# Router logits from the raw sums, gathers by four experts and three one-shot load places in a two-layer MoE block

## The chip, the cores and the metric

The kernel runs on one core of a Trainium2 chip. The metric is the device time of one execution in microseconds; 2232.28 us is the median of three runs of the kernel before (2230.65 to 2234.52).

## The reference, cut to what matters

256 tokens of 1024 channels go through a first block (half feed-forwards, neighbourhood attention with an mLSTM, spatial gating) and then through two layers of the block that the change touches. Each layer mixes the tokens, adds and normalises, sends every token to 2 of 16 experts, adds and normalises again:

```python
x = layer_norm_2(ALPHA * x + mix, ln_g[l, 0], ln_b[l, 0])
ffn = routed_moe(x, router_w, router_b, moe_w_gate[l], moe_w_up[l], moe_w_down[l])
x = layer_norm_2(ALPHA * x + ffn, ln_g[l, 1], ln_b[l, 1])

def routed_moe(x, ...):
    aff = sigmoid(xt @ router_w)                 # 256 x 16
    sel = aff + router_b                         # best of 4 groups of 4 experts, in it the top 2
    ...
    y = y + gates[:, e:e+1] * ((silu(xt @ w_gate[e]) * (xt @ w_up[e])) @ w_down[e])
```

`layer_norm_2` takes the mean and the variance over the 1024 channels, then gain and shift. Everything is f32.

## The kernel before

The tokens lie in two tiles t of 128, the channels in 8 blocks k of 128. A layer of the second block runs so.

**w_o projection** (`N.down`, `rows_out`, L184 to L187). The mixer's output times w_o, in split single-pass products, accumulates in four banks `yacc` (two halves n of 512 channels for each t). Tile 0's last matmuls come before tile 1's, 24 for each. For each finished tile `norm2` (L766) is called: DVE adds `x = ALPHA x + yacc` by halves (L772), gathers statistics (L773, L761), takes 1/sqrt by three steps of Newton (`rsq`, L216 to L225) and writes `xn` (L776).

**Router** (`moe`, L1081). PE transposes `xn` (L255). ACT (L1219, the first four k) and DVE (L1222, the last four) copy it out of PSUM as `xT` with gain and shift. `lg` (L1223) gives 16 x 256 logits, with the router's weights as the stationary operand. ACT takes the sigmoid (L1227), PE transposes back to token rows `pt` (L1230), and from `sel` (L1232) to `mask` (L1262) DVE selects in some 25 small steps. `rk` (L1266, L1267) counts ranks on PE, `r` (L1268) is the slot of every token at its expert, 64 slots (`CAP`) for each of the 16 experts.

**Gather.** `places` (L1095) writes the 0/1 matrix `Dg` for eight experts (512 columns), `gather` (L1105) multiplies the two halves `xrh`, `xrl` of `xn` (split at L97 on ACT and L98 on DVE) by it: 32 matmuls of 512 columns, each with a 128 x 128 weight load, and an eviction with gain and shift on ACT (L1107) for every k. The result for experts 0 to 7 goes into the place of the tile H (the mixer's input), that for experts 8 to 15 into the place of Y (the mixer's output). The first gather runs before the experts, the second within pair 1. L783 and L784 are the affine part of the norm, which the later sums need.

**Experts**, in eight pairs: 32 matmuls `pe` with gate and up weights (L1138, eight loads of 1 MB), then 32 `yp` with the down weights (L1169, four loads), whose result is scattered back (L1181, L1182) and added by DVE (L1183). After two chunks of pair 0, `back` computes the gates by slot and the transposed `Dg`.

**Loads.** `Loads` (L30) holds the 96 loads of a layer in their order of use. A place is filled when it opens, and again whenever PE has consumed it (`give`). The places open in four groups: M1 during the mixer (4 in layer 0, 2 in layer 1), M2 after the mixer (1, 3), M3 when the projection's weights are done (6), M4 in pair 2 (2). All loads are issued from SP's queue, in the order of the program.

The order on each engine is set by a scheduler, from the program's order; `tc.issue_after` pins an instruction behind another.

Of the kernel before, what the change touches and what calls it, by code (L numbers as in the profile page):

```python
# [19 lines left out]
KD = D // P  # L20
# [3 lines left out]
ALPHA = 4.0 ** 0.25  # L24
RAW, HL = 2, 4
CAP, NP = 64, 8
# [4 lines left out]
class Loads:  # L31
# [5 lines left out]

    def open(self, pool, n, late=True):

        self.free += [(pool, f"{pool.name}{i}", late) for i in range(n)]  # L40
        self.fill()

    def fill(self):
        while self.free and self.n < len(self.srcs):
            pool, tag, late = place = self.free.pop(0)
            if not late and self.n >= self.until:
                continue
            t = pool.tile([P, 2048], F32, name="mw", tag=tag, bufs=1)
            self.nc.sync.dma_start(t, self.srcs[self.n])
            self.got.append((t, place))  # L50
            self.n += 1

    def take(self):
        return self.got.pop(0)

    def give(self, got):
        self.free.append(got[1])
        self.fill()


class Net:
# [695 lines left out]
    def moments(self, t):  # L757
# [4 lines left out]
        v.tensor_scalar(mv[:, 2:3], mv[:, 1:2], 1e-5, None, ALU.add)  # L762
        return mv[:, 0:1], self.rsq(mv[:, 2:3])

    def norm2(self, x, t, y=None):

        v = self.nc.vector
        if y is not None:
            self.st[t] = self.sp.tile([P, 2, 6], F32, name="st2", tag="st2")
            for n in range(2):  # L770
                cs = slice(512 * n, 512 * n + 512)
                v.scalar_tensor_tensor(x[:, t, cs], x[:, t, cs], ALPHA, y[n], ALU.mult, ALU.add)  # L772
                v.bn_stats(out=self.st[t][:, n], in_=x[:, t, cs])  # L773
# [298 lines left out]
    def moe(self, x, l, mp, load, early, mixed, probe, ahead):  # L1072
# [6 lines left out]
        nc, A, tc = self.nc, self.A, self.tc  # L1079
        v, mm = nc.vector, nc.tensor.matmul  # L1080
        with ExitStack() as ctx:  # L1081
# [6 lines left out]
            xg = [None, None]  # L1088
# [3 lines left out]
            def places(h):  # L1092

                for t in range(NT):
                    v.tensor_tensor(Dg[:, t, 512 * h:512 * h + 512].rearrange("p (e s) -> p e s", s=CAP),  # L1095
                                    self.iota[:, 0:CAP].unsqueeze(1).to_broadcast([P, 8, CAP]),
                                    bc(r[:, t, 8 * h:8 * h + 8], CAP), ALU.is_equal)

            def gather(h, xr):

                xg[h] = mp.tile([P, KD, 512], F32, name="xg" + "HY"[h], tag="HY"[h])
                for k in range(KD):
                    ps = self.bank("D" if h else "AB", "pg")
                    for n, (a, t) in enumerate((a, t) for a in xr for t in range(NT)):
                        mm(ps, a[:, t, P * k:P * k + P], Dg[:, t, 512 * h:512 * h + 512], start=(n == 0),  # L1105
                           stop=(n == 2 * NT - 1))
                    last = nc.scalar.activation(xg[h][:, k], ps, AF.Identity, bias=self.lnc[:, l, 0, 1, k:k + 1],  # L1107
                                                scale=self.lnc[:, l, 0, 0, k:k + 1])
                return last

            def back():

# [15 lines left out]
            def pair_in(load, j, between=lambda: None):  # L1128

                pss = []  # L1130
                for tag in "AB":
                    ps = self.bank(tag, "pe")
                    for c in range(2):
                        ws = [load.take() for _ in range(2)]
                        for k in range(4):
                            for e, (w, _) in enumerate(ws):
                                b = CAP * e
                                mm(ps[b:b + CAP], xg[j // 4][:, 4 * c + k, P * (j % 4) + b:P * (j % 4) + b + CAP],  # L1138
                                   w[:, 512 * k:512 * k + 512], start=(c == 0 and k == 0), stop=(c == 1 and k == 3),
                                   tile_position=(0, b))  # L1140
# [55 lines left out]
            with ExitStack() as rt:  # L1196
# [4 lines left out]
                sc, sh = self.lnc[:, l, 0, 0], self.lnc[:, l, 0, 1]  # L1201
                lg = self.bank("A", "lg")
                xn = []
# [8 lines left out]
                pss = [[self.transposed([xn[t]], range(4 * g, 4 * g + 4), "BD"[t]) for g in range(2)] for t in range(NT)]  # L1212
                for t in range(NT):
                    for g in range(2):
                        xT = rp.tile([P, 4, P], F32, name="xT", tag="sg", bufs=2)
                        for q in range(4):
                            k = 4 * g + q
                            if g == 0:
                                nc.scalar.activation(xT[:, q], pss[t][g][q], AF.Identity, bias=sh[:, k:k + 1],  # L1219
                                                     scale=sc[:, k:k + 1])  # L1220
                            else:
                                v.tensor_scalar(xT[:, q], pss[t][g][q], sc[:, k:k + 1], sh[:, k:k + 1], ALU.mult, ALU.add)  # L1222
                            mm(lg[:16, P * t:P * t + P], self.rw[:, k], xT[:, q], start=(k == 0), stop=(k == KD - 1))  # L1223
                for t in range(NT):
                    self.split(xr[0][:, t], xr[1][:, t], xn[t])
                af = f("af", [16, T])
                nc.scalar.activation(af, lg[:16, :T], AF.Sigmoid)  # L1227
                pt = self.pa("pt")
                for t in range(NT):
                    nc.tensor.transpose(pt[:, 16 * t:16 * t + 16], af[:, P * t:P * t + P], self.ident[0:16, 0:16])  # L1230
                aff, sel = pt[:, :32].rearrange("p (t e) -> p t e", t=NT), f("sel", [P, NT, 16])
# [30 lines left out]
                v.tensor_tensor(mask, mask, o2, ALU.add)  # L1262
# [6 lines left out]
                places(0)  # L1269
                gather(0, xr)  # L1270
                places(1)
# [6 lines left out]
                for t in range(NT):  # L1278
                    self.affine(x, t, xn[t], gb, v)
                gb = self.ln_rows(l, 1)  # L1280

                def counts():
# [18 lines left out]
            with tc.If(left > 0):  # L1301
                with tc.tile_pool(name="r2", bufs=1) as rp:
                    xr = [rp.tile([P, NT, D], F32R, name=n) for n in ("xrh", "xrl")]
                    with tc.For_i(0, T // CAP - 1, 1):
                        for t in range(NT):
                            self.split(xr[0][:, t], xr[1][:, t], xn[t])
                        v.tensor_scalar(r, r, float(-CAP), None, ALU.add)
                        for h in range(2):
                            places(h)
                            gather(h, xr)  # L1310
# [405 lines left out]
```

## Time and profile before

| | |
|---|---|
| median of three runs | 2232.28 us |
| the profiled execution | 2237.53 us |
| its span | 2235.4 us |
| PE busy | 2085.6 us (93%) |
| DVE busy | 1283.9 us (57%) |
| ACT busy | 830.2 us (37%) |
| mean granted clock of PE | 0.968 |
| DMA over the span | 514.45 MB, 230 GB/s |

The span is the time from the first to the last instruction; the execution's own time lies 2.1 us above it. Shares of busy time are means over stages with different limits: the share of the DMA engines is 0.9 and more in the two expert stages (from about 1626 and 2030 us) and about a half over most of the rest. Matmuls are pipelined, so that PE counts as busy while it runs at less than its peak.

### The profile page before, as it was taken

How to read it: one execution, taken by the hardware profiler on the slowest of the kernel's cores; microseconds unless marked ns; L12 is line 12 of the kernel's file. 1: busy time of each engine (PE TensorE's matmuls, PEld its weight loads, DVE VectorE, ACT ScalarE, POOL GpSimd, SP SyncE). 2: the span in 40 equal slices, each digit the busy share in tenths (PEclk: the TensorE clock that was granted, in tenths of full speed). 3: DMA queues.
4: the chain of work that ended last, by engine and by line, in shares of the span. 5: the costliest groups of instructions: out<-in, count | busy, mean ns of one | idle time of the engine just before them, and what ended most of it. 6: DMA issues, size and time to landing. Idle time of an engine off the chain costs nothing. (4 is left out here: it accounts for less than half of the span.)

```text
span 2235.4 us, 30410 instructions
## 1 busy us (share of the span) xinstructions
PE 2085.6 (93%) x12028; PEld 1578.7 (71%) x12028; DVE 1283.9 (57%) x2554; ACT 830.2 (37%) x1441; POOL 65.6 (3%) x76
## 2 busy tenths in 40 slices
PE   6999999989989998999999999897999978989996
PEld 5878887876879997999997999785533347643332
DVE  5897637735578868876685655667011158631113
ACT  3222325434455444444554544453300026521000
POOL 0000000002000000000000000200000021100000
PEclk9999999999999999999999999899899989989999
DMA  8567634434248775885445554434599955359996
GB/s 323 202 238 276 244 113 151 119 118 59 76 154 318 288 280 200 291 296 193 151 170 207 210 206 151 182 114 170 226 404 421 422 222 186 136 203 392 420 421 251
DMA packets 94746, 514.45 MB, mean 230 GB/s; under 512 B 19648, under 2 KB 21056, under 8 KB 43520
## 3 DMA queue, kind: packets, MB, share of 16 engines
q1 hardware_dynamic: 88272, 502.34, 60.0%
q10 hardware_dynamic: 5168, 5.85, 0.9%
q0 software_dynamic: 1152, 4.19, 0.6%
q8 instruction: 98, 1.61, 0.3%
q14 instruction: 56, 0.46, 0.1%
HBM read 511.30 MB, written 1.05 MB: 229 GB/s over the span
## 5 line engine op out<-in xcount | busy, mean ns | idle before, releaser
L98 DVE TENSOR_TENSOR wlo<-raw,whi 128x1024 fp32r<-128x1024 f32 x421 | 514.1, 1232 | 280.9 <-ACT whi L97 278.5
L97 ACT CAST whi<-raw 128x1024 fp32r<-128x1024 f32 x421 | 434.9, 1048 | 608.5 <-PE pa L152 173.7
L152 PE MATMUL pa<-hh,whi 128*128 128x256 f32 (+1 forms) x720 | 222.5, 309 | 4.6 <-DVE hh L277 4.6
L152 PE MATMUL pa<-hl,whi 128*128 128x256 f32 (+1 forms) x720 | 221.5, 308 | 0.6 <-DVE hl L278 0.5
L152 PE MATMUL pa<-hh,wlo 128*128 128x256 f32 (+1 forms) x720 | 220.7, 307 | 0.0
L152 PE MATMUL pb<-hh,whi 128*128 128x256 f32 (+1 forms) x720 | 219.1, 304 | 0.0
L152 PE MATMUL pb<-hl,whi 128*128 128x256 f32 (+1 forms) x720 | 218.8, 304 | 0.0
L152 PE MATMUL pb<-hh,wlo 128*128 128x256 f32 (+1 forms) x720 | 218.7, 304 | 0.0
L355 DVE SCALAR_TENSOR_TENSOR macc<-rawm,cs,macc 128x512 f32<-128x512 f32 x266 | 193.2, 748 | 11.2 <-DMA rawm<-in_w_mod 6.9
L184 PE MATMUL yacc<-whi,gh 128*128 128x512 f32 x440 | 172.2, 396 | 1.3 <-ACT gate L375 1.3
L185 PE MATMUL yacc<-wlo,gh 128*128 128x512 f32 x440 | 171.2, 392 | 0.0
L152 PEld LDWEIGHTS pa<-hh,whi 128*128 128x128 f32 x720 | 138.2, 192 | 18.0 <-DVE hh L277 5.1
L1169 PE MATMUL yp<-mw,hT 128*64 128x512 f32 x512 | 139.5, 598 | 9.6 <-DMA mw<-in_w_dn 8.3
L152 PEld LDWEIGHTS pa<-hl,whi 128*128 128x128 f32 x720 | 138.3, 192 | 10.4 <-DVE hl L278 1.6
L1148 DVE SCALAR_TENSOR_TENSOR sg<-sg,gs,pe 128x512 f32<-128x512 f32 x16 | 12.0, 747 | 232.7 <-PE pe L1138 232.7
L152 PEld LDWEIGHTS pa<-hh,wlo 128*128 128x128 f32 x720 | 138.8, 193 | 6.6
L152 PEld LDWEIGHTS pb<-hh,wlo 128*128 128x128 f32 x720 | 136.7, 190 | 6.2
L152 PEld LDWEIGHTS pb<-hh,whi 128*128 128x128 f32 x720 | 136.5, 190 | 6.2
L152 PEld LDWEIGHTS pb<-hl,whi 128*128 128x128 f32 x720 | 136.3, 189 | 6.2
L187 PE MATMUL yacc<-whi,gl 128*128 128x512 f32 x440 | 140.4, 393 | 0.0
L1138 PE MATMUL pe<-mw,xgY 128*64 128x512 f32 x512 | 122.6, 597 | 8.7 <-DMA mw<-in_w_gu 8.7
L1138 PE MATMUL pe<-mw,xgH 128*64 128x512 f32 x512 | 122.8, 605 | 0.0
(457 smaller groups left out, 3628.0 us busy)
## 6 DMA issues: line engine op xcount, KB each, us to landing
mw<-in_w_gu SPq DMA_DIRECT2D x128, 1024.0 KB, 18.5
raw<-in_ffn_w_in SPq DMA_DIRECT2D x88, 1024.0 KB, 5.0
rawm<-in_w_mod SPq DMA_DIRECT2D x72, 1024.0 KB, 5.7
mw<-in_w_dn SPq DMA_DIRECT2D x64, 1024.0 KB, 19.8
raw<-in_ffn_w_out SPq DMA_DIRECT2D x55, 1024.0 KB, 5.0
raw<-in_mix_wT SPq DMA_DIRECT2D x8, 1024.0 KB, 4.9
raw<-in_sg_wR SPq DMA_DIRECT2D x8, 1024.0 KB, 4.9
raw<-in_sg_wT SPq DMA_DIRECT2D x8, 1024.0 KB, 4.8
```

What stands on the lines that cost most here:

```text
L97: self.nc.scalar.copy(hi, src)
L98: self.nc.vector.tensor_tensor(lo, src, hi.bitcast(F32), ALU.subtract)
L152: self.nc.tensor.matmul(o, w[:, k], h[:, k], start=(k == 0 and i == 0), stop=(k == nk - 1 and i == len(steps) - 1))
L184: mm(y[n], a, whi[:, cs[n]], start=first, stop=False)
L185: mm(y[n], a, wlo[:, cs[n]], start=False, stop=False)
L187: mm(y[n], b, whi[:, cs[n]], start=False, stop=last)
L355: v.scalar_tensor_tensor(o, raw[:, k], w, o, ALU.mult, ALU.add)
L1138: mm(ps[b:b + CAP], xg[j // 4][:, 4 * c + k, P * (j % 4) + b:P * (j % 4) + b + CAP], w[:, 512 * k:512 * k + 512], start=(c == 0 and k == 0 ...
L1148: v.scalar_tensor_tensor(sg, sg, gs[:, j:j + 1], pss[1], ALU.mult, ALU.mult)
L1169: mm(yp[n][b:b + CAP], hT[:, i, b:b + CAP], w[:, D * k + 512 * n:D * k + 512 * n + 512], start=(i == 0), stop=(i == 3), tile_position=(0, b))
```

## The change

The logits are computed from the raw sums `x = ALPHA x + y`, ahead of the norm. With m and rs a token's mean and 1/deviation, `lg = x (gain * rw)`, `cs` the column sums of `gain * rw` and `cb` those of `shift * rw`, the logits are `rs * lg - m * rs * cs + cb`. PE transposes each half of `x` as soon as it is summed, ACT copies four blocks at once, and the matmul gives token rows (128 x 16), so the transposes after the sigmoid go. `xn` is made for the gather alone. The low halves `xrl` are made in four pieces pinned behind other steps, and the affine part comes behind all the places. The gathers go by four experts: 0 before the experts, 1 in pair 1, 2 and 3 in pair 2, with two k in one bank. Gathers 0 and 1 go into Y, 2 and 3 into H. Until then both halves of H and the upper half of Y take one load each (`once`), which is not refilled.

```diff
+    def once(self, *tiles):
+        for t in tiles:
+            if self.n < len(self.srcs):
+                self.into(t, None)
...
     def give(self, got):
-        self.free.append(got[1])
-        self.fill()
+        if got[1]:
+            self.free.append(got[1])
+            self.fill()
...
+    def summed(self, x, t, y, then=lambda n: None):
...
+        for n in range(2):
+            cs = slice(512 * n, 512 * n + 512)
+            v.scalar_tensor_tensor(x[:, t, cs], x[:, t, cs], ALPHA, y[n], ALU.mult, ALU.add)
+            then(n)
+            v.bn_stats(out=self.st[t][:, n], in_=x[:, t, cs])
...
+            def places(q):
                 for t in range(NT):
+                    last = v.tensor_tensor(Dg[:, t, T * q:T * q + T].rearrange("p (e s) -> p e s", s=CAP),
+                                           self.iota[:, 0:CAP].unsqueeze(1).to_broadcast([P, 4, CAP]),
+                                           bc(r[:, t, 4 * q:4 * q + 4], CAP), ALU.is_equal)
+                return last
+            def gather(q, xr, tags="D"):
+                xg[q] = zone[q // 2][:, q % 2].rearrange("p (k n) -> p k n", k=KD)
                 for k in range(KD):
+                    if k % 2 == 0:
+                        pg = self.bank(tags, "pg")
+                    ps = pg[:, T * (k % 2):T * (k % 2) + T]
+                    for n, (t, a) in enumerate((t, a) for t in range(NT) for a in xr):
+                        mm(ps, a[:, t, P * k:P * k + P], Dg[:, t, T * q:T * q + T], start=(n == 0),
                            stop=(n == 2 * NT - 1))
+                    nc.scalar.activation(xg[q][:, k], ps, AF.Identity, bias=sh[:, k:k + 1], scale=sc[:, k:k + 1])
...
+                w2 = f("w2", [P, 2, KD, 16])
+                for i, a in enumerate((sc, sh)):
+                    v.tensor_tensor(w2[:, i], self.rw, bc(a, 16), ALU.mult)
...
+                mm(ps[:, :32], self.ones, ws2.rearrange("p i e -> p (i e)"), start=True, stop=True)
...
+                def scored(t, y):
+                    lt = lg[:, 16 * t:16 * t + 16]
+                    def logits(n):
...
+                            nc.tensor.transpose(ps[:, P * q:P * q + P], x[:, t, P * k:P * k + P], self.ident)
...
+                        nc.scalar.copy(xT, ps.rearrange("p (q m) -> p q m", q=4))
...
+                            mm(lt, xT[:, q], w2[:, 0, k], start=(k == 0), stop=(k == KD - 1))
+                    self.summed(x, t, y, logits)
+                    m, rs = self.moments(t)
...
+                    v.tensor_scalar(mr, m, rs, -1.0, ALU.mult, ALU.mult)
+                    v.scalar_tensor_tensor(z, cs2[:, 0], mr, cs2[:, 1], ALU.mult, ALU.add)
+                    v.scalar_tensor_tensor(z, lt, rs, z, ALU.mult, ALU.add)
+                    nc.scalar.activation(aff[:, t], z, AF.Sigmoid)
+                    box.append(v.tensor_scalar(xn[t], x[:, t], m, rs, ALU.subtract, ALU.mult).ins)
...
-                mixed(lambda t, y: xn.append(self.norm2(x, t, y)))
+                mixed(scored)
+                zone = [mp.tile([P, 2, 2048], F32, name="xg" + n, tag=n) for n in "YH"]
+                load.once(zone[1][:, 0], zone[1][:, 1])
                 load.open(room, M2[l])
+                load.once(zone[0][:, 1])
                 self.ws.close()
...
+                with tc.issue_after(box[1]):
+                    low(0, 0)
+                    low(0, 1)
...
+                with tc.issue_after(masked.ins):
+                    low(1, 0)
...
+                first = places(0).ins
+                with tc.issue_after(first):
+                    low(1, 1)
+                gather(0, xr, "AB")
...
+                with tc.issue_after(first):
+                    for q in range(1, 4):
+                        places(q)
+                    for t in range(NT):
+                        self.affine(x, t, xn[t], gb, v)
...
-                experts(load, True, {0: lambda: (back(), counts()), 1: lambda: gather(1, xr), 2: room_left})
+                experts(load, True, {0: lambda: (back(), counts()), 1: lambda: gather(1, xr),
+                                     2: lambda: (gather(2, xr), gather(3, xr), room_left())})
```

The scheduler turns this into another order. On SP, the queue of all loads, around the w_o loads of layer 0 (`raw` is a buffer of w_o, `mw` a load place, `xgH` and `xgY` the one-shot places); before:

```order
L128 DMA raw<-in_ev_wT 128x2048 x2
L128 DMA raw<-in_w_o 128x2x1024 x4
L49 DMA mw<-in_w_gu 128x2048 x12
L49 DMA mw<-in_w_dn 128x2048 x4
L49 DMA mw<-in_w_gu 128x2048 x8
```

and after the change:

```order
L136 DMA raw<-in_ev_wT 128x2048 x2
L136 DMA raw<-in_w_o 128x2x1024 x3
L50 DMA xgH<-in_w_gu 128x2048 x2
L136 DMA raw<-in_w_o 128x2x1024
L50 DMA mw<-in_w_gu 128x2048
L50 DMA xgY<-in_w_gu 128x2048
L50 DMA mw<-in_w_gu 128x2048 x8
L50 DMA mw<-in_w_dn 128x2048 x4
```

Two loads stand ahead of the last w_o and one into Y ahead of eight others.

On PE, from tile 0's last w_o matmuls on, layer 0 (`ptr` transposes, `lg` logits); before, where the projection ends (L187) and both tiles' logits follow:

```order
L184 MATMUL yacc<-whi,Y 128x512
L185 MATMUL yacc<-wlo,Y 128x512
L187 MATMUL yacc<-whi,Y 128x512
L255 MATMUL ptr<-ident,xn 128x128 x8
L1223 MATMUL lg<-xT,rw 16x128 x8
L255 MATMUL ptr<-ident,xn 128x128 x8
L1223 MATMUL lg<-xT,rw 16x128 x8
L1230 MATMUL pt<-ident,af 128x16 x2
```

and after the change, the same place of tile 0, some 20 matmuls before the projection's end:

```order
L195 MATMUL yacc<-whi,Y 128x512
L1239 MATMUL ptr<-ident,x 128x128 x4
L192 MATMUL yacc<-whi,Y 128x512
L1239 MATMUL ptr<-ident,x 128x128 x4
L1244 MATMUL lg<-w_14677,xT 128x16 x4
L193 MATMUL yacc<-wlo,Y 128x512
L195 MATMUL yacc<-whi,Y 128x512
L192 MATMUL yacc<-whi,Y 128x512
L1244 MATMUL lg<-w_14677,xT 128x16 x4
L193 MATMUL yacc<-wlo,Y 128x512
```

Tile 0's transposes and logits now lie between tile 1's w_o matmuls; the transposes back (`pt`) are gone.

On DVE, from the last steps of tile 1's norm to the start of the selection, layer 0; before:

```order
L784 TENSOR_TENSOR x<-x,ln_b 128x512
L224 TENSOR_SCALAR rq_t<-rq_u,rq_t 128x1
L783 TENSOR_TENSOR x<-xn,ln_g 128x512
L223 TENSOR_SCALAR rq_u<-rq_t,rq_h 128x1
L784 TENSOR_TENSOR x<-x,ln_b 128x512
L224 TENSOR_SCALAR rq_t<-rq_u,rq_t 128x1
L776 TENSOR_SCALAR xn<-x,mv_14846,rq_t 128x1024
L783 TENSOR_TENSOR x<-xn,ln_g 128x512 x2
L98 TENSOR_TENSOR xrl<-xn,xrh 128x1024
L1222 TENSOR_SCALAR xT<-ptr,lnc 128x128 x4
L784 TENSOR_TENSOR x<-x,ln_b 128x512 x2
L1232 TENSOR_TENSOR sel<-pt,rb 128x32
```

and after the change:

```order
L232 TENSOR_SCALAR rq_t<-rq_u,rq_t 128x1
L231 TENSOR_SCALAR rq_u<-rq_t,rq_h 128x1
L232 TENSOR_SCALAR rq_t<-rq_u,rq_t 128x1
L1248 TENSOR_SCALAR mr<-mv_14908,rq_t 128x1
L1252 TENSOR_SCALAR xn<-x,mv_14908,rq_t 128x1024
L1249 SCALAR_TENSOR_TENSOR z<-cs_14681,mr 128x16
L1256 TENSOR_TENSOR xrl<-xn,xrh 128x512
L1250 SCALAR_TENSOR_TENSOR z<-lg,rq_t,z 128x16
L1256 TENSOR_TENSOR xrl<-xn,xrh 128x512
L1274 TENSOR_TENSOR sel<-aff,rb 128x32
```

The affine steps (L783, L784) and the `xT` copies have left this stretch; two of the four half splits stand in it, with the two logit steps `z`.

## Rows read from the trace of the kernel before

**Rows 1.** Busy by stretch: length; PE, PEld, DVE, ACT, POOL; clock, DMA share, GB/s.

```profile
1557.00:1584.00 27.00, 20.41 (x79) 12.22 (x77) 8.76 (x37) 7.88 (x10) 0.53 (x1) 0.77 0.17 55
1618.00:1625.00 7.00, 7.00 (x34) 2.30 (x32) 0.00 (x0) 0.67 (x1) 0.00 (x0) 1.00 0.51 181
1626.00:1806.00 180.00, 168.19 (x692) 57.79 (x690) 31.59 (x48) 15.90 (x27) 0.00 (x0) 1.00 1.01 422
2022.00:2031.00 9.00, 9.00 (x43) 3.36 (x44) 0.73 (x1) 1.56 (x2) 0.00 (x0) 1.00 0.63 233
```

**Rows 2.** PE in order of time (start, length), projection's end to experts, layer 0.

```profile
1543.98 0.39 PE L187 MATMUL yacc<-whi,Y 128*128 128x512 f32 x1
1545.94 1.09 PE L255 MATMUL ptr<-ident,xn 128*128 128x128 f32 x8 [1.57 <-DVE xn L776]
1547.42 2.27 PE L1223 MATMUL lg<-xT,rw 128*16 128x128 f32 x16 [0.39 <-issue]
...
1566.78 1.65 PE L1105 MATMUL pg<-Dg,xrh 128*128 128x512 f32 x3 [1.00 <-DVE Dg L1095]
...
1577.10 7.09 PE L1138 MATMUL pe<-mw,xgH 128*64 128x512 f32 x32
```

**Rows 3.** The same of PE in layer 1.

```profile
1951.90 0.40 PE L187 MATMUL yacc<-whi,Y 128*128 128x512 f32 x1
...
1973.87 1.62 PE L1105 MATMUL pg<-Dg,xrh 128*128 128x512 f32 x3 [1.10 <-DVE Dg L1095]
...
1983.77 0.65 PE L1138 MATMUL pe<-mw,xgH 128*64 128x512 f32 x2
```

**Rows 4.** DVE in order of time, norm's chain to sel, layer 0.

```profile
1541.09 0.21 DVE L761 BATCH_NORM_AGGREGATE mv<-st 128x2 f32<-128x12 f32 x1
...
1544.35 0.21 DVE L224 TENSOR_SCALAR rq_t<-rq_u,rq_t 128x1 f32<-128x1 f32 x1
1544.48 0.68 DVE L772 SCALAR_TENSOR_TENSOR x<-x,yacc 128x512 f32<-128x512 f32 x1
...
1552.50 0.81 DVE L776 TENSOR_SCALAR xn<-x,mv,rq_t 128x1024 f32<-128x1024 f32 x1
...
1559.65 0.19 DVE L1232 TENSOR_TENSOR sel<-pt,rb 128x32 f32<-128x32 f32 x1 [1.40 <-PE pt L1230]
```

**Rows 5.** DVE's groups by line and shape, 1544.4 to 1559.7 us: busy, mean ns.

```profile
L1222 DVE TENSOR_SCALAR xT<-ptr,lnc 128x128 f32<-128x128 f32 x8 | 2.9, 399 | 0.0
...
L98 DVE TENSOR_TENSOR xrl<-xn,xrh 128x1024 fp32r<-128x1024 f32 x2 | 2.4, 1218 | 0.0
```

**Rows 6.** ACT's groups by line and shape, 1544.4 to 1580 us.

```profile
L1107 ACT ACTIVATE xgH<-pg,lnc 128x512 f32<-128x512 f32 x8 | 6.2, 778 | 12.5 <-PE pg L1105 12.5
...
L97 ACT CAST xrh<-xn 128x1024 fp32r<-128x1024 f32 x2 | 2.1, 1047 | 16.6 <-DVE xn L776 16.6
...
L1227 ACT ACTIVATE af<-lg 16x256 f32<-16x256 f32 x1 | 0.4, 373 | 2.8 <-PE lg L1223 2.8
```

**Rows 7.** The first gather's first half, busy by stretch (columns as in rows 1).

```profile
1566.70:1572.60 5.90, 5.82 (x14) 4.56 (x15) 1.93 (x5) 1.85 (x3) 0.00 (x0) 0.50 0.00 0
```

**Rows 8.** PE in a steady stream of 256-column matmuls, first and last of 19.

```profile
702.82 0.28 PE L152 MATMUL pa<-hh,whi 128*128 128x256 f32 x1
...
704.94 0.28 PE L152 MATMUL pa<-hh,whi 128*128 128x256 f32 x1
```

**Rows 9.** PE at layer 0's second gather: first row, next expert's.

```profile
1609.51 0.74 PE L1105 MATMUL pg<-Dg,xrh 128*128 128x512 f32 x2
...
1617.78 7.09 PE L1138 MATMUL pe<-mw,xgH 128*64 128x512 f32 x32
```

**Rows 10.** The readers of the tile H between 1870 and 1880 us, layer 1.

```profile
L152 PE MATMUL pj<-H,wlo x16: 276/279/367, 1870.3 to 1874.5; 128*128 128x256 f32 x16
```

**Rows 11.** Layer 1's mixer and projection by stretch (columns as in rows 1).

```profile
1900.00:1930.00 30.00, 29.32 (x152) 19.10 (x151) 20.59 (x103) 18.86 (x67) 7.78 (x13) 0.99 0.10 36
1930.00:1952.00 22.00, 22.00 (x98) 16.41 (x96) 11.90 (x27) 7.82 (x13) 0.00 (x0) 1.00 0.64 240
```

More of the change, by code (lines that the diff above doesn't have):

```diff
@@ L38, in open, with into @@
     def open(self, pool, n, late=True):
-        self.free += [(pool, f"{pool.name}{i}", late) for i in range(n)]
+        self.free += [((pool, f"{pool.name}{i}"), late) for i in range(n)]
         self.fill()
+    def once(self, *tiles):
+        for t in tiles:
+            if self.n < len(self.srcs):
+                self.into(t, None)
+    def into(self, t, place):
+        self.nc.sync.dma_start(t, self.srcs[self.n])
+        self.got.append((t, place))
+        self.n += 1
     def fill(self):
         while self.free and self.n < len(self.srcs):
[L45 to L51, printed above, removed]
+            (pool, tag), late = place = self.free.pop(0)
+            if late or self.n < self.until:
+                self.into(pool.tile([P, 2048], F32, name="mw", tag=tag, bufs=1), place)
     def take(self):
@@ L763, in moments @@
         return mv[:, 0:1], self.rsq(mv[:, 2:3])
+    def summed(self, x, t, y, then=lambda n: None):
+        v = self.nc.vector
+        self.st[t] = self.sp.tile([P, 2, 6], F32, name="st2", tag="st2")
+        for n in range(2):
[3 more added lines that the diff above has]
+            v.bn_stats(out=self.st[t][:, n], in_=x[:, t, cs])
     def norm2(self, x, t, y=None):
@@ L768, in norm2 @@
         if y is not None:
[L769 to L773, printed above, removed]
+            self.summed(x, t, y)
         m, r = self.moments(t)
@@ L1087, in moe @@
             of, over = op.tile([1, 2], F32, name="of"), op.tile([1, 1], I32, name="over")
-            xg = [None, None]
+            xg = [None] * 4
             bc = lambda a, n: a.unsqueeze(len(a.shape)).to_broadcast(list(a.shape) + [n])
             sp = ctx.enter_context(tc.tile_pool(name="moes", bufs=2))
-            def places(h):
+            sc, sh = self.lnc[:, l, 0, 0], self.lnc[:, l, 0, 1]
+            def places(q):
                 for t in range(NT):
-                    v.tensor_tensor(Dg[:, t, 512 * h:512 * h + 512].rearrange("p (e s) -> p e s", s=CAP),
-                                    self.iota[:, 0:CAP].unsqueeze(1).to_broadcast([P, 8, CAP]),
-                                    bc(r[:, t, 8 * h:8 * h + 8], CAP), ALU.is_equal)
@@ L1099, in gather @@
-            def gather(h, xr):
-                xg[h] = mp.tile([P, KD, 512], F32, name="xg" + "HY"[h], tag="HY"[h])
-                for k in range(KD):
-                    ps = self.bank("D" if h else "AB", "pg")
-                    for n, (a, t) in enumerate((a, t) for a in xr for t in range(NT)):
-                        mm(ps, a[:, t, P * k:P * k + P], Dg[:, t, 512 * h:512 * h + 512], start=(n == 0),
+                    last = v.tensor_tensor(Dg[:, t, T * q:T * q + T].rearrange("p (e s) -> p e s", s=CAP),
+                                           self.iota[:, 0:CAP].unsqueeze(1).to_broadcast([P, 4, CAP]),
+                                           bc(r[:, t, 4 * q:4 * q + 4], CAP), ALU.is_equal)
@@ L1200, in moe @@
                 gb = self.ln_rows(l, 0)
-                sc, sh = self.lnc[:, l, 0, 0], self.lnc[:, l, 0, 1]
-                lg = self.bank("A", "lg")
-                xn = []
+                w2 = f("w2", [P, 2, KD, 16])
+                for i, a in enumerate((sc, sh)):
+                    v.tensor_tensor(w2[:, i], self.rw, bc(a, 16), ALU.mult)
+                ws2, cs2 = f("ws2", [P, 2, 16]), f("cs2", [P, 2, 16])
+                for i in range(2):
+                    v.tensor_reduce(ws2[:, i], w2[:, i].rearrange("p k e -> p e k"), AX.X, ALU.add)
@@ new lines, in moe @@
+                ps = self.bank("A", "cs2")
+                mm(ps[:, :32], self.ones, ws2.rearrange("p i e -> p (i e)"), start=True, stop=True)
+                v.tensor_copy(cs2.rearrange("p i e -> p (i e)"), ps[:, :32])
+                aff = f("aff", [P, NT, 16])
+                lg = self.bank("A", "lg")
+                xn = [self.sp.tile([P, D], F32, name="xn", tag="xn") for t in range(NT)]
+                def scored(t, y):
+                    lt = lg[:, 16 * t:16 * t + 16]
+                    def logits(n):
+                        ps = self.bank("BD"[t], "ptr")
+                        for q in range(4):
+                            k = 4 * n + q
+                            nc.tensor.transpose(ps[:, P * q:P * q + P], x[:, t, P * k:P * k + P], self.ident)
+                        xT = rp.tile([P, 4, P], F32, name="xT", tag="xT", bufs=2)
+                        nc.scalar.copy(xT, ps.rearrange("p (q m) -> p q m", q=4))
+                        for q in range(4):
+                            k = 4 * n + q
+                            mm(lt, xT[:, q], w2[:, 0, k], start=(k == 0), stop=(k == KD - 1))
+                    self.summed(x, t, y, logits)
+                    m, rs = self.moments(t)
+                    z, mr = self.sp.tile([P, 16], F32, name="z", tag="z"), self.sp.tile([P, 1], F32, name="mr", tag="mr")
+                    v.tensor_scalar(mr, m, rs, -1.0, ALU.mult, ALU.mult)
[3 more added lines that the diff above has]
+                    box.append(v.tensor_scalar(xn[t], x[:, t], m, rs, ALU.subtract, ALU.mult).ins)
@@ L1211, in moe @@
                 load.open(more.enter_context(tc.tile_pool(name="m3", bufs=1, side="right", reuse_waits="tile")), M3, False)
-                pss = [[self.transposed([xn[t]], range(4 * g, 4 * g + 4), "BD"[t]) for g in range(2)] for t in range(NT)]
                 for t in range(NT):
[L1214 to L1231, printed above, removed]
+                    nc.scalar.copy(xr[0][:, t], xn[t])
+                with tc.issue_after(box[1]):
+                    low(0, 0)
+                    low(0, 1)
+                sel = f("sel", [P, NT, 16])
                 v.tensor_tensor(sel, aff, self.rb.unsqueeze(1).to_broadcast([P, NT, 16]), ALU.add)
@@ L1277, in moe @@
                 v.tensor_tensor(gates, o1, bc(ws, 16), ALU.mult)
-                for t in range(NT):
-                    self.affine(x, t, xn[t], gb, v)
+                with tc.issue_after(first):
[3 more added lines that the diff above has]
+                        self.affine(x, t, xn[t], gb, v)
                 gb = self.ln_rows(l, 1)
@@ L1307, in moe @@
                         v.tensor_scalar(r, r, float(-CAP), None, ALU.add)
-                        for h in range(2):
-                            places(h)
-                            gather(h, xr)
+                        for q in range(4):
+                            places(q)
+                            gather(q, xr)
                         back()
```

14 lines of the change are left out of this document (6 added, 8 removed).

## The prediction

> **What bounds the kernel now.** I read the DMA share by stretches first, then PE and DVE in order of time from the end of the w_o projection to the first expert matmul, then the groups of one price.
>
> The two expert stages are bound by their loads. From 1626 to 1806 us the DMA engines are full (share 1.01) and move 422 GB/s [rows 1]; a load of 1024 KB then takes 2.49 us. Layer 1 has the same stage from 2032. PE has about 12 us to spare in those 180 us (168.2 busy). Before that the DMA engines stand nearly still: 0.17 of 1557 to 1584, because every early place is filled and none comes free until PE has consumed the first weights. One more hole lies at 1618 to 1625 (0.51 busy, so 3.4 us idle) and at 2022 to 2031 (0.63, 3.3 us). After this last hole nothing but the remaining loads counts. So the end of a layer moves by what the end of its last hole moves, and a hole ends when PE consumes a place: what brings PE forward up to there is gain, what happens to PE afterwards is not, unless it opens a new hole.
>
> PE is late because of the router. The last w_o matmul begins at 1543.98; the gather's first (pg) at 1566.78, the experts' first (pe) at 1577.10 [rows 2]. That is 22.4 us of router and 10.3 us of gather; in layer 1 21.6 and 9.9 [rows 3]. In the router DVE is the engine that is waited for: it takes the last sum x at 1544.48 and reaches sel only at 1559.65 [rows 4]. Between lie the gain-and-shift copies xT (8 of 0.40), two splits xrl of 1.22 [rows 5] and the affine steps of x, wedged between the links of the norm's chain.
>
> **The change, part by part.**
>
> Logits of tile 0 within the projection. Eight transposes and eight logit matmuls now stand between the last w_o matmuls. The same eight transposes took 1.09 us [rows 2]. The logits are 16 records: the old form (128 columns) took 2.27 for its 16 [rows 2], an upper end; the new form streams 16 columns but loads a weight tile each, so at least as long as the transposes. I take 1.8, and 0.2 for a wait on ACT's copies (0.78 each, as the eviction of the same size) [rows 6]. The projection ends later by **+3.1** (2.2 to 4.5). The column sums are one small matmul earlier and some DVE work while DVE waits for w_o: nothing, covered by the w_o loads; without that cover about 1 us.
>
> From the projection's end to sel. After the change: the sum 0.6 and statistics 0.65 (such a step shows 0.68 and overlaps its neighbour a little [rows 4]), the chain from AGGREGATE to the last rq_t, mr 0.2 and xn 0.8, then z, half a split, the logit step and ACT's sigmoid. The chain takes 3.47 us in the trace, with two other steps inside it [rows 4]; without them 2.3 to 2.45. PE's transposes, ACT's copy and the logits of this half run beside it (about 2.5 us against the 3.7 of statistics and chain). ACT casts xrh when xn is there (1.05) and only then takes the sigmoid (0.37) [rows 6], so sel comes 1.65 after xn; the two small steps (some 0.2 each, like the aggregate) and the half split (0.6) run under the cast. Together **6.3** where it was 15.3 (1544.4 to 1559.65). Gone from this path are the eight xT, both affine steps, one and a half splits, the transposes back to token rows. They are not gone from DVE: affine stands behind all the places, a half split beside rk on PE, another behind the first places. From sel to pg (7.1 now) I take 7.0: the first places are half as wide, and a half split is added that runs beside rk.
>
> So pg starts at −22.4 + 6.3 + 7.0 + 3.1 = **−6.0** us in layer 0, and −5.2 in layer 1, whose router was 0.8 shorter.
>
> Gather by four experts. The first gather streams 256 columns instead of 512. PE comes out of an idle stretch: for 5.9 us from 1566.7 the granted clock was 0.50 (1.2 GHz), 14 matmuls of 512 columns, 0.42 each [rows 7]. At half the columns 0.21; 27 of 32 fit into those 5.9 us, the other five go at the full level, where a 256-column stream runs at 0.118 (19 starts, the last 2.12 us after the first) [rows 8], and one pe slips in. 6.9 us instead of 10.3 and 9.9: **−3.4 and −3.0**. The first pe then comes 9.4 and 8.2 us earlier.
>
> Gather(1), inside the hole's stretch. It takes PE 8.3 us now (1609.51 to 1617.78) [rows 9]. At 256 columns 32 × 0.118 = 3.8, at most 5 with pe between and evictions. It comes 3.3 to 4.5 us shorter, as much as the last hole is long. More than the hole cannot be gained: **−3.4 and −3.3**.
>
> Gather(2) and (3) move into pair 2: 64 × 0.118 = 7.6 us that PE did not spend there, up to 11 if it waits for ACT. The loads issued ahead of PE there cover most of it; no row shows how much, so from nothing to 3 us of new hole, and I take **+1** for each layer, nearer to nothing because the shares behind the present hole show no idle time at all.
>
> The three one-shot places. They let three more loads land before PE starts, but they are never refilled. Once PE has consumed them, the loads issued are as before: those consumed and eleven more. The last hole comes after that. So **0**; at most 3 × 2.49 us a layer, if the stage followed the total loaded early. On SP's queue the six loads of M3 now stand behind the one into the upper half of Y, which waits for the projection's end: at 7 × 2.49 after 1547.5, and the way of the first, they are in by about 1567.5, as PE starts; their consumers come after the first eight loads. The two into H stand ahead of the last w_o (in layer 1 ahead of the last three and the last two). H is last read at 1874.5 in layer 1 [rows 10], and the projection begins at 1930 (98 matmuls in the 22 us from there) [rows 11], so 0.
>
> The odd mixer of layer 1 comes out in another order on DVE, ACT and PE though its code is untouched: 0, with ±3 us, as PE is busy 29.3 of 30 us there [rows 11].
>
> **The sum.** Layer 0: −6.0 −3.4 −3.4 +1 = −11.8. Layer 1: −5.2 −3.0 −3.3 +1 = −10.5. Together −22.3, on the profiled execution 2237.5 → 2215.2. It ran 5.25 above the median of the runs shown, 2232.28, so I forecast **2210**.
>
> Weight loads, the one price in doubt. Four gathers need 128 weight loads a layer where two needed 64. From 702.8 to 704.9, 256-column matmuls that change their weights each time start every 0.118 us [rows 8], hence I price the loads at nothing. The Trainium skill ("TensorE: Matmul & The Clock Gate", section "LDWEIGHTS (loading the stationary operand)") gives a load columns/1.2 ns, an estimated 107 ns here. Were it all exposed, by that page gather(1) would take about 7 us and gathers (2) and (3) about 14. The rows speak against that for a steady stream.
>
> **Rivals.**
>
> Exposed weight loads, as a mechanism of this kernel: the operand order now changes the stationary tile with every matmul and two k share a bank, so a stream could run at the cold spacing, 0.21, throughout. Gather(1) then gains 1.5 of the 3.4, gathers (2) and (3) cost 13.5 and open a hole of some 3: about −6 a layer, 2220. The rows of the steady stream speak against it.
>
> Stalls: the logits wait for ACT's copies inside the projection, and pair 2's detour drains the load queue. Both upper ends (+1.4 and +2 a layer) give −15.5: about 2217. For it: PE obeys its order strictly. Against: PE has slack in every pair.
>
> The early places count in full: 7.5 us more a layer, 2195. For it: DMA is the bound of the stage. Against: the hole.
>
> Slower: in layer 1, SP waits in order. If the reordered mixer frees H later, the w_o loads behind the two into H are late. H is free at 1874.5; a w_o that is issued after about 1925 delays the projection, us for us. To cancel the 22.3, H must be freed after about 1947; freed at 1957 it would give 2242. The untouched code and 50 us of room speak against it.
>
> The change does nothing: if the loads bound the stage from its start, a shorter router only lengthens the wait for weights: 2232. The 0.17 share before PE starts speaks against it.
>
> **How the numbers follow.** The forecast 0.57; stalls 0.20; exposed loads 0.05; early places 0.08; another gain outside these (router chain yet shorter, or half the gain lost) 0.04; nothing 0.02; slower 0.04. The unknown costs alone give 2203 (no new hole, mixer −3, chain 1 us shorter a layer) to 2218; with the stalls and the exposed loads 2221. So **2202 to 2221**, which leaves out under 2 in 10. A change under 0.2% (4.5 us) could not be told from none. Faster 0.94, same 0.02, slower 0.04.
>
> **Signs.** Right: first pe near 1567.7 and 1975.5; sel about 6.3 us after the last w_o matmul, which itself is 3 us later; pg spaced 0.21 at clock 0.50, then 0.12; gather(1) in 4 to 5 us and no DMA hole behind it; loads into H issued as soon as it is read (1875 in layer 1), the one into Y at the projection's end. Wrong: a hole in pair 2 of over 3 us; pg spaced 0.2 at full clock; w_o late in layer 1; or a layer that shortens by much more than its first pe and its last hole.

## The result: slower by 0.7%, and the profile after

The change takes 2246.95 us (median of five, 2243.05 to 2251.15) against 2231.4 (five runs, 2229.55 to 2234.52): a ratio of 1.0069, with a 95% interval of 1.0051 to 1.0086. The forecast was 2210, faster.

The profiled execution after (span 2244.8 us) is its kernel's median; the one before (2235.4) took 2237.5 us, 6.1 above the median of the five. So the profiles differ by 9.4 us where the medians differ by 15.6. The 9.4 lie in places far apart. From PE's rows in order of time and from the landings of the loads:

| stretch | before, us | after, us | difference |
|---|---|---|---|
| start to the first w_o matmul of layer 0 | 1514.2 | 1531.5 | +17.3 |
| from there to layer 0's last recorded landing of an expert load | 289.9 | 285.5 | −4.4 |
| on to the first w_o matmul of layer 1 | 97.9 | 96.1 | −1.8 |
| from there to layer 1's last landing | 310.4 | 308.9 | −1.5 |
| to the end | 23.0 | 22.8 | −0.2 |

The router and the first gather did nearly what they were meant to. PE of the changed kernel in order of time (start, length), layer 0, answering [rows 2]:

```profile
1531.53 0.58 PE L192 MATMUL yacc<-whi,Y 128*128 128x512 f32 x1
...
1564.11 0.40 PE L195 MATMUL yacc<-whi,Y 128*128 128x512 f32 x1
...
1577.61 0.58 PE L1123 MATMUL pg<-Dg,xrh 128*128 128x256 f32 x1 [0.74 <-DVE Dg L1110]
...
1582.56 1.32 PE L1154 MATMUL pe<-mw,xgY 128*64 128x512 f32 x2
...
1585.41 1.08 PE L1154 MATMUL pe<-mw,xgY 128*64 128x512 f32 x4
```

From the end of the projection (1564.11 and 0.40) to pg are 13.1 us where there were 22.4. The first pe stands 51.0 us after the first w_o matmul where it stood 62.9; two pe lie inside the gather, and the stream of pe behind it starts 53.9 us after. In layer 1 the first pe comes after 70.2 us where it came after 81.8. DVE of the changed kernel, from tile 1's last sum, answering [rows 4]:

```profile
1564.55 0.69 DVE L779 SCALAR_TENSOR_TENSOR x<-x,yacc 128x512 f32<-128x512 f32 x1
...
1568.49 0.80 DVE L1252 TENSOR_SCALAR xn<-x,mv,rq_t 128x1024 f32<-128x1024 f32 x1
...
1570.70 0.19 DVE L1274 TENSOR_TENSOR sel<-aff,rb 128x32 f32<-128x32 f32 x1
...
1575.53 0.19 DVE L1304 TENSOR_TENSOR mask<-mask,o 128x32 f32<-128x32 f32 x1
```

The loss in the layers comes later. Busy time by stretch of the changed kernel (columns as in [rows 1]):

```profile
1622.00:1630.00 8.00, 8.00 (x40) 3.10 (x40) 0.54 (x1) 1.54 (x4) 0.00 (x0) 1.00 0.71 269
1658.40:1667.00 8.60, 8.60 (x48) 4.43 (x50) 0.75 (x1) 3.10 (x6) 0.00 (x0) 1.00 0.26 83
1667.00:1810.00 143.00, 134.61 (x554) 45.93 (x552) 23.12 (x35) 11.78 (x20) 0.00 (x0) 1.00 1.01 420
2058.00:2070.00 12.00, 12.00 (x68) 6.18 (x68) 0.75 (x1) 4.14 (x8) 0.00 (x0) 1.00 0.32 111
```

The hole behind the second gather has not gone (0.29 of 8 us, 2.3; by the gap between landings, less 2.49 us for each load in it, 2.9 us in layer 0, where it was 2.6). In pair 2 there is a new one: 1658.4 to 1667.0 with the DMA engines busy for 0.26, and in layer 1 2058 to 2070 with 0.32. By the landings they are 7.6 and 8.8 us long. Behind them the engines are full again. What SP's queue waited for in that stretch (engine, line, us in total, times, longest):

```profile
SPq L50 <- PE pg L1123: 15.6, 1, 15.6
SPq L50 <- PE pe L1154: 9.7, 4, 6.7
```

For 15.6 us, from 1648.0 to 1663.6, SP stood before one load, the first of M4's places, whose memory is that of xrh and xrl until the fourth gather has read them. The places that PE freed in that time were refilled only then.

The 17.3 us at the head lie in code that the change does not touch; 15 of them arise between 669 us, where the two kernels still stand within 0.5 us of each other, and the end of the last feed-forward's first half (1384.6 and 1400.0 us). One step of the last feed-forward, its 48 matmuls of 256 columns, first and last row; before:

```profile
1359.98 0.28 PE L152 MATMUL pa<-hh,whi 128*128 128x256 f32 x1
...
1365.33 0.28 PE L152 MATMUL pb<-hh,wlo 128*128 128x256 f32 x1
```

and after:

```profile
1374.54 0.28 PE L160 MATMUL pa<-hh,whi 128*128 128x256 f32 x1
...
1380.12 0.28 PE L160 MATMUL pb<-hh,wlo 128*128 128x256 f32 x1
```

47 intervals in 5.35 us and in 5.58: 0.1139 us against 0.1187, with the clock granted in full both times:

```profile
1240.00:1392.00 152.00, 152.00 (x1119) 143.14 (x1118) 84.69 (x96) 70.91 (x96) 0.00 (x0) 1.00 0.57 201
```

```profile
1251.00:1408.00 157.00, 157.00 (x1120) 147.60 (x1119) 84.66 (x97) 70.64 (x95) 0.00 (x0) 1.00 0.53 193
```

The same stage (1119 matmuls, 1120 after) takes 152 us before and 157 after, and PE alone is busy throughout. (PEld, the weight loads, runs beside PE.)

### The profile page after: what moved, and what is told of

It reads as the page before. It is cut to its first block, busy times and chain, and to the rows that moved or that the text cites. A ratio compares the mean times of both kernels' runs of the same rounds, so it can differ in the third digit from the quotient of the medians.

```text
span 2244.8 us, 30723 instructions
## 1 busy us (share of the span) xinstructions
PE 2103.6 (94%) x12156; PEld 1598.4 (71%) x12156; DVE 1285.5 (57%) x2572; ACT 836.4 (37%) x1467; POOL 65.8 (3%) x76
## 5 line engine op out<-in xcount | busy, mean ns | idle before, releaser
L363 DVE SCALAR_TENSOR_TENSOR macc<-rawm,cs,macc 128x512 f32<-128x512 f32 x266 | 193.2, 749 | 13.1 <-DMA rawm<-in_w_mod 9.1
```

Of the source, the lines that this page charges most:

```text
L363: v.scalar_tensor_tensor(o, raw[:, k], w, o, ALU.mult, ALU.add)
```

## The experiments

Two theories were put forward for the two losses. **Placement**: the two new scratch tiles z and mr come from the low pool `sp`, and their 192 bytes a partition push up every buffer that is allocated above it, in the first block too. **SP's queue**: M4's load blocks the refills in pair 2. Their rivals: the first block is slow by chance or for another reason; PE's detour of 64 gather matmuls is itself the hole.

### e1: the scratch tiles in the router's pool

```diff
-  z, mr = self.sp.tile([P, 16], ...), self.sp.tile([P, 1], ...)
+  z, mr = (rp.tile([P, w], F32, name=m, tag=m, bufs=2) for m, w in (("z", 16), ("mr", 1)))
```

> The change with its two new scratch tiles z and mr (192 bytes a partition) taken from the router's own pool instead of the pool that lies below nearly everything; the same instructions in the same order. Theory 'placement': every later buffer is back at its address of before, the first block loses its 17 us (the first w_o matmul at 1514 us instead of 1531.5), and the whole is near 2247 - 17 = 2230, the same as before. Rival 'the first block is slow for another reason' (the added program, a chance of the runs): the w_o start stays at 1531 and the time at 2247.

Measured: 2229.88 us, ratio to before 0.9983 (0.9969 to 0.9996). The first w_o matmul stands at 1508.2 (the profiled kernels with the low pool as in before have it at 1508 to 1514, those with 192 bytes more in it at 1529 to 1533). The step of the feed-forward:

```profile
1355.09 0.28 PE L160 MATMUL pa<-hh,whi 128*128 128x256 f32 x1
...
1360.44 0.28 PE L160 MATMUL pb<-hh,wlo 128*128 128x256 f32 x1
```

0.1139 us again, with the change's instructions in the change's order. Placement holds.

### e2: the kernel before, with 192 empty bytes

```diff
         self.sp = pool("sp", 2)
+        self.sp.tile([P, 48], F32, name="pad", tag="pad", bufs=1)
```

> The kernel before with nothing but an unused tile of 192 bytes a partition in that low pool. Theory 'placement': the first w_o matmul comes near 1531 instead of 1514 and the time near 2231 + 17 = 2248, a little less where w_o itself runs faster. Rival: no change, 2231.

Measured: 2254.35 us, ratio 1.009 (1.0067 to 1.0112), w_o at 1532.5. The step:

```profile
1374.31 0.28 PE L153 MATMUL pa<-hh,whi 128*128 128x256 f32 x1
...
1379.89 0.28 PE L153 MATMUL pb<-hh,wlo 128*128 128x256 f32 x1
```

0.1186 us. An unused tile alone costs 20 us by the medians, more than the whole change. The rival falls.

### e3 and e4: M4 in pair 3

```diff
-  2: lambda: (gather(2, xr), gather(3, xr), room_left())})
+  2: lambda: (gather(2, xr), gather(3, xr)), 3: room_left})
```

> The change with the two late load places of M4 opened in pair 3 instead of pair 2, the scratch tiles where the change has them. Theory 'SP stands still': the load into M4 no longer waits in SP's queue for the last gather with the freed places behind it; the DMA holes of 7.6 and 8.8 us in pair 2 go, and the time falls by 12 to 16 us to 2231-2235. Rival 'the detour': the 64 gather matmuls in pair 2 keep PE from consuming weights and the hole stays, 2245-2249.

> Both edits together. If both theories hold, 2247 - 17 - 14 = 2216, 15 us under the kernel before and 0.7%; if only the placement holds 2230; if only the queue holds 2233; if neither, 2247.

Measured: e3 (scratch tiles as in the change) 2241.74 us, ratio 1.0032 (1.0018 to 1.0045); e4 (with e1's edit) 2219.98 us, 0.994 (0.992 to 0.9961). SP's waits in e4 in the same part of pair 2, and its DMA share there and in layer 1:

```profile
SPq L50 <- PE pe L1154: 26.1, 8, 8.2
SPq L50 <- PE yp L1185: 5.7, 5, 2.2
```

```profile
1640.00:1650.00 10.00, 10.00 (x56) 5.00 (x56) 0.75 (x1) 3.10 (x6) 0.00 (x0) 1.00 0.76 274
2037.00:2048.00 11.00, 11.00 (x58) 5.10 (x58) 0.75 (x1) 3.64 (x8) 0.00 (x0) 1.00 0.69 263
```

The wait for pg is gone, and the holes shrink to 2.4 us (0.24 of 10) and 3.4 (0.31 of 11). Against e1 the layers end 3.7 us sooner each by the landings. So SP's queue held, but for 5 us (e3 against the change) to 10 (e4 against e1) and not 12 to 16. What is left of the hole I put down to the rival, PE's detour: SP's longest wait there is now 8.2 us for pe, and e8, which halves the detour, has no hole in pair 2 of layer 0.

### e5: other shifts, on e4

```diff
+        self.sp.tile([P, 16], F32, name="pad", tag="pad", bufs=1)   (32, 8 in the others)
```

> The version with both edits (scratch tiles moved, M4 in pair 3) and an unused tile of 64 bytes a partition in the low pool. If the place modulo 128 bytes decides, 64 is the same place as the change's 192: the 256-column matmuls of the first block start every 0.119 us and the time is near 2220 + 17 = 2237. If it is modulo 256 or more, this shift may cost less, 2220 to 2230.

> The same with 128 bytes. If the place modulo 128 decides: no change, 0.114 us and 2220. If any shift from the layout of before costs: 2237.

> The same with 32 bytes: the buffers above come to lie on multiples of 64 bytes, the weight buffers on the far side of the memory stay 32 off. If only the distance between the two sides matters, somewhere between 2210 and 2240; no theory gives it better.

Measured, in this order (64, 128, 32 bytes): 2237.94 us (1.0027, 1.0009 to 1.0044), 2232.92 (1.0008, 0.9993 to 1.0024) and 2239.17 (1.0025, 1.001 to 1.0039), 13 to 19 us above e4. Median intervals between starts, in ns, for the feed-forward's 256-column matmuls (1300 to 1400 us), the 512-column ones of its second half, and those of w_o:

| shift, bytes | 256 columns | 512 columns | w_o |
|---|---|---|---|
| 0 (e4) | 113 | 229 | 234 |
| 32 | 117 | 233 | 234 |
| 64 | 120 | 227 | 232 |
| 128 | 118 | 233 | 229 |
| 192 (e2) | 119 | 231 | 227 |

Modulo 128 does not decide: 128 bytes cost as well. No shift is best for all three. The two 512-column series look like one: each has 227 at one shift (64 bytes for the feed-forward, 192 for w_o), 229 at 64 bytes less, 231 or 232 at 128 bytes off, and 233 or 234 at the others. That fits a place modulo 256 bytes (for w_o, shift 0 then lies 64 bytes above 192). No trace shows the addresses themselves, and five shifts fit more than one rule.

### e6: without the one-shot places

```diff
-                load.once(zone[1][:, 0], zone[1][:, 1])
...
-                load.once(zone[0][:, 1])
```

> The version with both edits without the three one-shot places. My forecast gave these places nothing: the last DMA hole comes after they are used up, so 2220 (2216 to 2224). Rival 'the loads landed early count in full': up to 7.5 us a layer slower, 2235. On SP the six loads of M3 then no longer stand behind the one into Y.

Measured: 2220.6 us, 0.9946 (0.9929 to 0.9963), as e4. By the times the three early places are worth nothing, as forecast; a few us could hide in the intervals. They are not without effect, though. The stretch behind the second gather in layer 0, in e4 and here:

```profile
1600.00:1610.00 10.00, 10.00 (x53) 4.89 (x54) 0.00 (x0) 3.09 (x6) 0.00 (x0) 1.00 0.76 300
```

```profile
1608.00:1618.00 10.00, 10.00 (x47) 3.19 (x43) 0.94 (x2) 0.58 (x1) 0.00 (x0) 1.00 1.00 383
```

Without the early places the hole of layer 0 is gone, as the forecast had it for the change, and in layer 1 1.4 us of it remain; with them the load before the hole lands sooner (in layer 0 92.5 us after the first w_o matmul in e4, 97.4 here) and holes of 2.8 and 2.0 us remain. By the landings layer 0 ends 2.5 us later here than in e4, layer 1 0.8 sooner.

### e7 and e8: what the gather by four is worth, and spreading it

e7 goes back to the gathers by eight experts and to M4 in pair 2, drops the one-shot places, and keeps the router, with e1's edit. e8 is e4 with

```diff
-  2: lambda: (gather(2, xr), gather(3, xr)), 3: room_left})
+  2: lambda: gather(2, xr), 3: lambda: gather(3, xr), 4: room_left})
```

> The change's router alone: logits on raw sums, low halves and affine part in their new places, scratch tiles in the router's pool, but the gathers by eight experts (the second in pair 1), no one-shot places and M4 in pair 2, all as before. Theory 'the gather by four gives back in pair 2 what it brings ahead of the experts': the first pe comes some 8.5 us after that of the version by four only by 3.5, the hole behind the second gather stays, none opens in pair 2; 8 to 9 us a layer to the end, 2234 - 17 = 2217 (2213 to 2221). Rival 'the gather by four is worth its 6 us a layer': 2226.

> The version with both edits, the third gather in pair 2, the fourth in pair 3, M4 in pair 4. If the 16 us that PE spends between two pieces of pair 2 drain the places, two visits of 8 us leave no hole of over 1 us and the time falls by 3 to 6 us to 2214-2217. Rival: M4's two places, now open a pair later, are what is missing, and it stays at 2220 or rises to 2223.

Measured: e7 2218.51 us, 0.9942 (0.9922 to 0.9963); e8 2218.79, 0.9934 (0.9909 to 0.996). e7's first pe comes 55.8 us after the first w_o matmul, e4's 50.9; yet layer 0 ends 281.4 us after it in e7 and 281.0 in e4, layer 1 304.7 and 304.9. The hole behind the second gather is there in e7 too (by the landings 2.6 us in layer 0), and there is none in pair 2:

```profile
1608.00:1618.00 10.00, 10.00 (x50) 3.43 (x48) 0.75 (x1) 0.00 (x0) 0.00 (x0) 1.00 0.68 261
1620.00:1660.00 40.00, 39.68 (x174) 13.80 (x172) 8.56 (x13) 4.71 (x8) 0.00 (x0) 1.00 1.01 421
```

The gather by four brings PE forward and gives all of it back in pair 2. Spread over two pairs it comes out the same: the hole of pair 2 is gone, one of 2.8 us opens in pair 3 in layer 0. By the landings e8's layer 1 is 2.5 us shorter than e4's, but the stretch from layer 0's end to layer 1's first w_o matmul, whose code is the same, is 3.6 us longer, so the times cannot tell the two.

### e9 to e12: placing by rule

e9 is e4 with empty tiles below H (128 bytes), Y (64) and the feed-forward's gh (64). e10 is e8 with the first two alone, e12 is e7 with them, e11 the kernel before with the third alone. The third, and the first two:

```diff
         with self.tc.tile_pool(name="ffn", bufs=2) as fp:
             gs = []
+            fp.tile([P, 16], F32, name="pad", tag="pad", bufs=1)
...
+                for n, w in (("H", 32), ("Y", 16)):
+                    bp.tile([P, w], F32, name="pad" + n, tag="pad" + n)
+                    both.append(bp.tile([P, 2, KD, T], F32R, name=n, tag=n))
```

> The version with both edits, with 128 bytes of nothing below H, 64 more below Y and 64 below the feed-forward's gh. From the runs with 0, 32, 64, 128 and 192 bytes: 256-column matmuls start every 0.1135 us where the streamed operand lies 64 bytes below the stationary one modulo 256, 0.118 to 0.120 elsewhere; 512-column ones every 0.227 where both lie alike, 0.229 to 0.234 elsewhere. If that rule holds: the projections out of H go from 0.118 to 0.1135, those of w_o from 0.233 to 0.227, gh's from 0.229 to 0.227, 5 to 6 us together, 2214. Rival, no such rule: any cadence may come, and the time is above 2220.

> The version with the third and fourth gathers spread over pairs 2 and 3, and the two empty pieces below H and Y alone (128 and 64 bytes), gh where it was. Theory 'gh's place sets the feed-forward's cadence': its 256-column matmuls are back at 0.1135-0.115 us; the projections out of H at 0.114 and w_o at 0.227 stay; 2218 - 3.6 = 2215. Rival 'the pieces below H and Y did it': 0.118 and 2223.

> The kernel before with 64 empty bytes below gh and gl in the feed-forward's pool and nothing else moved. Theory 'gh's place': the 256-column matmuls, whose own operands stay where they are, go from 0.115 to 0.118 us, the 512-column ones from 0.229 to 0.227; some 7 us slower, 2238-2240. Rival: 0.115 stays, 0.227 comes, 2 us faster.

> The change's router with the gathers by eight experts, and the empty pieces below H and Y: 2218.5 - 3.6 = 2215, as the spread version, if the gather by four is worth nothing to the end of the layer.

Measured: e9 2227.89 us (0.9977, 0.9963 to 0.9992), e10 2219.19 (0.9928, 0.9907 to 0.9949), e11 2239.3 (1.0024, 1.0012 to 1.0037), e12 2219.47 (0.9924, 0.9901 to 0.9947). The 512-column cadences that the rule named came: w_o 227 in e9, e10 and e12, gh's 227 in e9 and e11. H's projections ran at 113 or 114 ns in most of their groups and at 118 in the others (6 of 8 in e9; in e4 1 of 8). But in e9 the feed-forward's 256-column matmuls went to 118, though by the order of allocation neither of their operands had moved, and e11 shows that 64 bytes in the pool of gh, gl and the scratch tile sa do this alone. Its step:

```profile
1365.50 0.28 PE L152 MATMUL pa<-hh,whi 128*128 128x256 f32 x1
...
1371.03 0.28 PE L152 MATMUL pb<-hh,wlo 128*128 128x256 f32 x1
```

0.1178 us against 0.1139 before, in the same instructions, with 64 bytes moved under the operand of the *other* matmuls. So the cadence is not set by the places of a matmul's own two operands alone. e10 and e12 missed too, with 2215 expected: faster w_o and H matmuls gained no time over e8 and e7.

## Why the prediction was wrong

**Right, by its own steps.** The projection's lengthening: from its first matmul to its last 32.6 us where there were 29.7, +2.9 with w_o's faster cadence in it; in e4, where w_o's cadence is nearly that of before, 32.9, +3.2 (forecast +3.1). Projection to sel: 6.2 (6.3). Sel to pg: 6.9 (7.0). First gather: 7.8 us with two pe in it, which take 1.3 (forecast 6.9 with one); it runs at 0.21 us a matmul at first, then at 0.118. Gather(1): from 1616.4 to 1624.0, of which 3 us are pe, so 4.5 (3.8 to 5). The weight loads are not exposed; two rows of that gather, six starts apart:

```profile
1616.64 0.28 PE L1123 MATMUL pg<-Dg,xrl 128*128 128x256 f32 x1
...
1617.34 0.28 PE L1123 MATMUL pg<-Dg,xrl 128*128 128x256 f32 x1
```

0.117 us with a load each. The rule of the Trainium skill ("TensorE: Matmul & The Clock Gate", section "LDWEIGHTS (loading the stationary operand)"), taken as added time, does not show here: with it this gather would have taken the 7 us that the prediction estimated. At the last old hole, load 25 of 96, the kernel was 13.7 us ahead of before in layer 0, counted from the first w_o matmul, and 10.8 in layer 1; the forecast's terms up to there were 12.8 and 11.5.

One sign missed in this part: "no DMA hole" behind gather(1). The hole stayed, and e6 shows the one-shot places behind that, which the sum had at nothing. Without them the hole is gone in layer 0 and half gone in layer 1, and the lead there is 11.9 and 11.2 us, so the terms themselves held; that the lead came out near the forecast with the places and the hole in it is in part luck.

**Wrong, the step of gathers (2) and (3).** "+1 for each layer", from nothing to 3 us, priced PE's detour alone. Behind it in the same pair stands the opening of M4, and its load waits for the last gather in an in-order queue, with the refills behind it. I listed the queue for w_o and for M3 and not for M4. By load 37 the lead had fallen from 14.0 to 6.2 us in layer 0 and, at load 35, from 12.5 to 3.5 in layer 1. Without that wait (e4) 2.4 and 3.4 us of hole remain, about the upper end of my range. The prediction's sign "a hole in pair 2 of over 3 us" told the failure; the rival "Stalls" had the place, at 2 us a layer more and not 7 to 8. The rival "Slower: in layer 1, SP waits in order" had the mechanism, but at w_o, which was not late.

**Wrong, a term that the sum did not have.** "On the profiled execution 2237.5 → 2215.2" takes all that lies outside the change as it was. 192 bytes of new tiles in a pool below everything else cost 17 us by the medians (the change against e1; the layers take as long in both profiles, within 1 us), where the sum had 22.3 to win. No row of before shows what another placement costs, as only one had been run. A hint was there: the steady stream of [rows 8], at 703 us, ran at 0.118 us a matmul, the step at 1359.98 at 0.1139, in the same kernel.

Put together: −4.4 −1.5 in the layers instead of −11.8 and −10.5, −1.8 from layer 0's last landing to layer 1's first w_o matmul, which holds the mixer (0 ± 3), and +17.3.

Two slips in the working changed no conclusion. The terms of the rival "Exposed weight loads" (−6.0 −3.4 −1.5 and a hole of 3) add to −7.9 and, in layer 1, −6.7, which gives 2218 and not 2220. The sign "first pe near 1975.5" leaves out what layer 0 was to gain.

**What is left.** With the low pool as in before, the router's edits alone gain 0.6 (e7) to 0.8% (e12, with the pieces below H and Y), and with the gather by four, spread, 0.7% (e8, e10): 2218.5 to 2219.5 us, all faster than both kernels. None of these four is told apart from another.

## What to carry to other kernels

Before a new tile goes into a pool that others are stacked on, look at what it moves; where PE's stream is the bound, a kernel with nothing but an unused tile of that size tells the cost in a few runs. A place whose memory is released by work in the same stage must not be filled from the queue that feeds that stage; and work that is taken off a start but has to be done before the loads settle has only been put off. Where a prediction sums differences, ask which part of the kernel it holds constant, and whether the change does.

## What was not expected of the hardware

The start-to-start time of a matmul changes with where buffers lie: 113 to 120 ns for 256 columns, 227 to 234 for 512, at a full granted clock, with the order of instructions unchanged (e2, e5, e9, e11). It stays the same whether ACT and DVE are busy or not: in the change, between 600 and 1420 us, 118.8 ns on average with both idle and 118.8 with DVE's split running and ACT idle. The Trainium skill ("TensorE: Matmul & The Clock Gate", section "Back-to-back issue gap") gives columns/2.4 and 2.5 ns for an isolated matmul at the full clock, an estimated 109 for 256 columns, and names no place of the operands there; the measurement decides, and it is above that at every placement.

For 256 columns the place is not all, either. The kernel before has two cadences with the same buffers. The step of [rows 8] began at 702.82 and its 48th matmul stands here, followed by the same step in e1, first and last row:

```profile
708.36 0.28 PE L152 MATMUL pb<-hh,wlo 128*128 128x256 f32 x1
```

```profile
700.85 0.28 PE L160 MATMUL pa<-hh,whi 128*128 128x256 f32 x1
...
706.20 0.28 PE L160 MATMUL pb<-hh,wlo 128*128 128x256 f32 x1
```

5.54 us for 47 intervals, 0.1179, and 5.35, 0.1138. There are 51 such steps of 48 matmuls between 600 and 1420 us. With the feed-forward's buffers where before has them (before, e1, e4, e6, e7, e8, e10, e12) 38 to 46 of them run at 0.114 and all the others at 0.118, and which ones differs from profile to profile. With these buffers or gh shifted (the change, e2, e3, e5, e9, e11) none of the 51 runs faster than 0.1177, in any of eight profiles. So e11's 0.1178 is no new cadence but the slower one of before, and a shift of gh keeps these steps out of the faster one. In e9 and e11 the faster one still comes in some opening matmuls of a feed-forward, before the feed-forward has read its gh (median 0.113 over the 96 from 669 us on).

What sets the cadence stays open: no trace shows addresses, and e11 shows that 64 bytes in the pool of gh, gl and sa count, not by which tile.
